# Gate-and-up weights split 256 columns at a time: products in pairs of PSUM banks, two of the four weight sums made by adding DMAs

## The chip, the core and the metric

The kernel runs on one core of one Trainium2 chip. The metric is the device time of one execution in microseconds, median of several runs. The engines are named as the profile names them: PE (TensorE matmul) with PEld (its weight load), DVE (VectorE), ACT (ScalarE), POOL (GpSimd) and SP (SyncE, which here only issues DMAs).

## What is computed

One layer of a decoder trunk on 512 tokens of width 1024, all in float32: a SwiGLU sub-layer with half weight, a mixer (causal pooling beside sliding-window attention), and a second SwiGLU sub-layer with half weight. Each sub-layer stands between two RMS norms.

```python
def swiglu(h, w_gu, w_down):
    gate, up = jnp.split(h @ w_gu, 2, axis=-1)
    return (jax.nn.silu(gate) * up) @ w_down

h = swiglu(rms_norm(x, ffn1_pre), ffn1_w_gu, ffn1_w_down)      # w_gu 1024 x 5632, w_down 2816 x 1024
x = x + 0.5 * rms_norm(h, ffn1_post)
h = token_mixer(rms_norm(x, mix_pre), cos, sin, w_in, w_pool, pool_scale, sinks, g_pool, g_attn, w_out)
x = x + rms_norm(h, mix_post)
h = swiglu(rms_norm(x, ffn2_pre), ffn2_w_gu, ffn2_w_down)
x = x + 0.5 * rms_norm(h, ffn2_post)
```

## The kernel before

**Matmuls from split operands.** Every float32 operand is split into a high part of 12 significant bits and the rest, its low part, and `mm3` (L301) makes one product from three matmuls (high by high, high by low, low by high). A split costs one copy for the high part (L125 on ACT or L127 on DVE) and one subtraction for the low part (L128, on DVE or POOL).

**Weights.** The class `Weights` (L94) holds two lists in order of use: `loads`, which SP carries out as DMAs of 512 KB into eight rotating buffers (`big`), and `todo`, the operands that are split out of them. `get(name)` (L139) splits everything up to that operand and `AHEAD` = 4 further ones; `more(n)` splits the next n, `put(hi, lo)` the next one on the engines named, and each split first sees that `run_ahead` more loads have been issued. Before the change nearly every operand is 128 partitions by 512 elements: half of a load. The pool for split weights has `WB` = 12 pairs of such tiles.

**Gate and up** (`gate_up`, L441). The 2816 columns of gate and of up are taken in eleven chunks of 256 columns (`CH`). The first chunk (c = 0) is done plainly, in eight blocks: `block(i)` for half of the tokens, gate or up, and each 128 columns; its weights are eight operands (L161 to L166), one for each of gate/up, 128 columns and half of the features. For the blocks 0 to 3 and everything that is called between them (`between`: `first_steps` L599 in the first sub-layer, `last_steps` L1115 in the second) PE, DVE, ACT and POOL keep the order of the program (`in_order`, L81). `first_steps` splits all eight operands by `put`. In the second sub-layer the last `W.more(4)` of `output` (L1094) splits the first four, and four `put`s in `last_steps` (L1120 to L1125) the other four.

The other ten chunks use seven products instead of eight of the two by two blocks (Winograd's form of Strassen's), for 128 columns at a time (`for j in range(2)`, L491): each product is twelve matmuls of 256 tokens. The operands are the four blocks of weights and four sums of them: `a11` makes two of the sums (L181, L182), `s2` (L187) and `s4` (L192) one each, on DVE; for chunk 1 POOL makes those of `a11`. The sums of tokens are made once (`token_sums`, L400). PE goes through the products 1, (4 of the block before), 2, 5, 6, 3, 7. Results are evacuated by ACT (L497, L505, L507, the silu L510) and DVE (L503, L509, L512, L484, L485). `behind` (L435) lets the splits of an operand follow the last evacuation on their engine.

**Down** (`down_proj`, L523) runs k over 22 blocks of 128 rows, with all eight PSUM banks as accumulators; the mixer and its output projection (`mixer` L938, `output` L1077) follow in an order written out by hand.

**PSUM** is one pool of eight banks (`bank`, L84).

Of the kernel before, what the change touches and what calls it, by code (L numbers as in the profile page):

```python
# [15 lines left out]
ALU = mybir.AluOpType  # L16
# [23 lines left out]
WB = 12  # L40
AB = 8
HB = 25
BIG = 8
AHEAD = 4
# [4 lines left out]
def shape_consts():  # L49
    """What depends on the shapes alone: the band of the sliding window, the count of tokens at the  # L50
    start of a trailing window, and the frequencies of the rotation."""
    c = np.zeros((P, CW), np.float32)
    i, j = np.arange(P)[:, None], np.arange(2 * P)[None, :]
    diff = i + P - j
    c[:, :256] = np.where((diff >= 0) & (diff < P), 0.0, NEG)
    for g, w in enumerate(WINDOWS):
        n = np.minimum(np.arange(16) + 1, w)
        c[:, 256 + 16 * g : 272 + 16 * g] = (np.float32(w) / n.astype(np.float32))[None, :]
    e = -np.arange(0, ROT, 2, dtype=np.float32) / np.float32(ROT)
    c[:, -8:] = np.power(np.float32(500000.0), e)[None, :]  # L60
    return c
# [3 lines left out]
def trunk_layer(  # L65
# [11 lines left out]
    pp = ctx.enter_context(tc.tile_pool(name="pp", bufs=8, space=PSUM))  # L77
# [6 lines left out]
    def bank(name):  # L84
        return pp.tile([P, 512], F32, tag="ps", name=name)
# [7 lines left out]
    # ---- weights, in the order of their use: each is split into two parts of 12 significant bits  # L93
    class Weights:  # L94
        def __init__(self):
# [3 lines left out]
            self.hi, self.lo = nc.scalar, nc.vector  # L99

        def add_load(self, key, src, shape):
            self.loads.append((key, src if isinstance(src, list) else [(slice(0, P), src)], shape))

        def add(self, name, make):
            """An operand: make() gives it in float32 once the loads added so far are there."""
            self.index[name] = len(self.todo)
            self.todo.append((name, len(self.loads), make))

        def load_to(self, n):
            while self.loaded < min(n, len(self.loads)):  # L110
                key, src, shape = self.loads[self.loaded]
                self.raw[key] = big(f"{key}_raw", shape)
                for at, part in src:
                    nc.sync.dma_start(self.raw[key][at], part)
                self.loaded += 1

        def make_to(self, n):
            while self.made < min(n, len(self.todo)):
                name, need, make = self.todo[self.made]
                self.load_to(need + self.run_ahead)  # L120
                src = make()
                hi = wp.tile(list(src.shape), F32R, tag="hi", name=f"{name}_hi")
                lo = wp.tile(list(src.shape), F32R, tag="lo", name=f"{name}_lo")
# [4 lines left out]
                self.lo.tensor_tensor(lo, src, hi.bitcast(F32), ALU.subtract)  # L128
                self.parts[name] = (hi, lo)
# [15 lines left out]
    def add_plain(key, src, shape, picks):  # L145
        W.add_load(key, src, shape)
        for name, at in picks:
            W.add(name, lambda at=at: W.raw[key][at])

    def add_gate_up(name, w_gu, c):  # L150
        def load(m, kh):
            c0 = m * FF + c * CH
            src = w_gu[0, kh * 512 : (kh + 1) * 512, c0 : c0 + CH]
            W.add_load(f"{name}_{c}{m}{kh}", src.rearrange("(k p) c -> p k c", p=P), [P, 4, CH])

        cut = [(slice(None), slice(None), slice(j * P, (j + 1) * P)) for j in range(2)]
        if c == 0:
            for m in range(2):
                load(m, 0)
                load(m, 1)  # L160
                for i in range(4):  # L161
# [3 lines left out]
                        lambda m=m, kh=kh, j=j: W.raw[f"{name}_0{m}{kh}"][cut[j]],  # L165
                    )  # L166
            return
        for m in range(2):
            for kh in range(2):
                load(m, kh)  # L170
        box = {}

        def parts(j):
            return [W.raw[f"{name}_{c}{m}{kh}"][cut[j]] for m in range(2) for kh in range(2)]

        def a11(j):
            r = parts(j)
            if j == 0:
                box["s1"] = big(f"{name}_{c}s1", (P, 4, CH))
            eng = nc.gpsimd if c == 1 else nc.vector  # L180
            eng.tensor_tensor(box["s1"][cut[j]], r[2], r[3], ALU.add)  # L181
            eng.tensor_tensor(r[2], r[0], r[2], ALU.subtract)  # L182
            return r[0]

        def s2(j):
            r = parts(j)
            nc.vector.tensor_tensor(r[0], box["s1"][cut[j]], r[0], ALU.subtract)  # L187
            return r[0]

        def s4(j):  # L190
            r = parts(j)
            nc.vector.tensor_tensor(r[1], r[1], r[0], ALU.subtract)  # L192
            return r[1]

        makers = (
            (1, a11), (2, lambda j: parts(j)[1]), (5, lambda j: box["s1"][cut[j]]), (6, s2), (3, s4),
            (7, lambda j: parts(j)[2]), (4, lambda j: parts(j)[3]),
        )
        for j in range(2):
            for p, make in makers:  # L200
                W.add(f"{name}_{c}{j}p{p}", lambda make=make, j=j: make(j))

    def add_ffn(name, w_gu, w_down):
        for c in range(NCH):
            add_gate_up(name, w_gu, c)
        for k in range(KF):
            add_plain(
                f"{name}_d{k}", w_down[0, k * P : (k + 1) * P, :], [P, D],
                [(f"{name}_d{k}{n}", (slice(None), slice(n * 512, (n + 1) * 512))) for n in range(2)],
            )  # L210

    def add_in(name, c0, w, kk, per):
        for q in range(KD // kk):
            src = w_in[0, q * kk * P : (q + 1) * kk * P, c0 : c0 + w]
            picks = [
                (f"{name}{(q * kk + i) // per}", (slice(None), i if per == 1 else slice(i, i + per)))
                for i in range(0, kk, per)
            ]
            add_plain(f"{name}_{q}", src.rearrange("(k p) c -> p k c", p=P), [P, kk, w], picks)

    # ---- what stays on chip
# [20 lines left out]
    rows = cp.tile([12, P], F32, name="rows")  # L242
# [7 lines left out]
    add_in("wq", PW, 512, 2, 1)  # L250
    add_in("wkv", 2 * PW, 256, 4, 2)
    add_in("wu", 0, 512, 2, 1)
    for n in range(2):
        ns = slice(n * 512, (n + 1) * 512)
        for q in (2, 3, 0, 1):
# [6 lines left out]
            picks = [(f"wo{n}{2 * q + i}", (slice(None), i)) for i in range(2)]  # L262
            add_plain(f"wo{n}_{q}", src, [P, 2, 512], picks)
# [12 lines left out]
    def power(ms, name):  # L276
        """ms ** -0.5"""
# [23 lines left out]
    def mm3(ps, wl, xr, first, last, open_=False):  # L301
        """ps += w.T @ x from the parts of both."""
# [10 lines left out]
    # ---- norm of a block of tokens, and its transpose  # L313
# [37 lines left out]
    def post_norm(t, parts, g, scale, name, dst=None):  # L351
        """x += scale * norm(parts) * g for a block of tokens."""
# [30 lines left out]
    def evacuate(src, t, kh, xq):  # L383
        at = slice((t % 2) * P, (t % 2 + 1) * P)
        hi, lo = xq[0][kh, t // 2]
        nc.scalar.copy(hi[:, :, at], src)
        nc.vector.tensor_tensor(lo[:, :, at], src, hi[:, :, at].bitcast(F32), ALU.subtract)

    def keep(src, t, kh, xq):
        at = slice((t % 2) * P, (t % 2 + 1) * P)  # L390
        for q in range(2):
            nc.scalar.copy(xq[1][kh, t // 2][q][:, :, at], src[:, 2 * q : 2 * q + 2, :])
# [7 lines left out]
    def token_sums(xq, name):  # L400
        """The sums of quarters that the seven products take."""
# [5 lines left out]
        for q in range(2):  # L407
            b11, b12, b21, b22 = (full[i][q] for i in ((0, 0), (0, 1), (1, 0), (1, 1)))
            nc.vector.tensor_tensor(b11, b12, b11, ALU.subtract)
            nc.vector.tensor_tensor(b12, b22, b12, ALU.subtract)  # L410
            nc.vector.tensor_tensor(b22, b22, b11, ALU.subtract)
            nc.vector.tensor_tensor(b21, b21, b22, ALU.subtract)
# [754 lines left out]
```

## Time and profile before

The profile is that of one execution on the core. A page shows the busy time of each engine; the timeline view lists instructions in order of time, merged where alike, with the idle time before them in brackets and what ended it; the windows view gives the busy time of each engine in each stretch.

| | |
|---|---|
| median of 3 runs | 871.87 us (870.04 to 873.93) |
| the profiled execution: its span from first to last instruction | 871.8 us |
| ACT busy | 428.1 us (49%) |
| POOL busy | 104.6 us (12%) |
| first sub-layer: gate and up; down | to about 242 us; 242 to about 360 us |
| mixer and output projection | about 360 to 516 us |
| second sub-layer: gate and up; down | about 516 to 745 us; 745 to 864 us |
| moved by DMA | 87.35 MB, mean 100 GB/s |

A span of 871.8 us and a median of 871.87 us say that the profiled execution is an ordinary one.

### The profile page before, as it was taken

How to read it: one execution, taken by the hardware profiler on the slowest of the kernel's cores; microseconds unless marked ns; L12 is line 12 of the kernel's file. 1: busy time of each engine (PE TensorE's matmuls, PEld its weight loads, DVE VectorE, ACT ScalarE, POOL GpSimd, SP SyncE). 2: the span in 40 equal slices, each digit the busy share in tenths (PEclk: the TensorE clock that was granted, in tenths of full speed). 3: DMA queues.
4: the chain of work that ended last, by engine and by line, in shares of the span. 5: the costliest groups of instructions: out<-in, count | busy, mean ns of one | idle time of the engine just before them, and what ended most of it. 6: DMA issues, size and time to landing. Idle time of an engine off the chain costs nothing. (4 is left out here: it accounts for less than half of the span.)

```text
span 871.8 us, 14391 instructions
## 1 busy us (share of the span) xinstructions
PE 848.6 (97%) x5633; PEld 775.9 (89%) x5633; DVE 628.8 (72%) x1177; ACT 428.1 (49%) x923; POOL 104.6 (12%) x124
## 2 busy tenths in 40 slices
PE   7999999999999999999989989999999999999996
PEld 5999999999988888888767779999999999888885
DVE  6988888888893223855998879988888888942214
ACT  6555555555583222637653356555555555832211
POOL 4300000000000000136464334000000000000000
PEclk9999999999999999999999999999999999999999
DMA  9333333333363333202023401333333333642002
GB/s 306 89 97 98 97 98 97 111 118 127 105 232 122 97 97 95 73 26 51 24 64 108 143 24 50 97 98 97 98 97 97 108 119 114 227 135 73 1 1 97
DMA packets 62448, 87.35 MB, mean 100 GB/s; under 512 B 3492, under 2 KB 50220, under 8 KB 62380
## 3 DMA queue, kind: packets, MB, share of 16 engines
q1 hardware_dynamic: 62380, 86.44, 31.0%
q8 instruction: 44, 0.72, 0.3%
q14 instruction: 24, 0.20, 0.1%
HBM read 84.33 MB, written 2.10 MB: 99 GB/s over the span
## 5 line engine op out<-in xcount | busy, mean ns | idle before, releaser
L304 PE MATMUL f_acc<-f_d_hi,f_hp_hi 128*128 128x512 f32 x352 | 137.4, 390 | 0.0
L306 PE MATMUL f_acc<-f_d_hi,f_hp_lo 128*128 128x512 f32 x352 | 137.1, 389 | 0.0
L305 PE MATMUL f_acc<-f_d_lo,f_hp_hi 128*128 128x512 f32 x352 | 137.1, 389 | 0.0
L128 DVE TENSOR_TENSOR f_d_lo<-f_d_raw,f_d_hi 128x512 fp32r<-128x512 f32 x88 | 58.9, 690 | 100.4 <-ACT f_d_hi L125 100.4
L125 ACT CAST f_d_hi<-f_d_raw 128x512 fp32r<-128x512 f32 x88 | 53.2, 621 | 108.6 <-PE f_acc L306 107.2
L304 PEld LDWEIGHTS f_acc<-f_d_hi,f_hp_hi 128*128 128x128 f32 x352 | 66.1, 188 | 13.7
L306 PEld LDWEIGHTS f_acc<-f_d_hi,f_hp_lo 128*128 128x128 f32 x352 | 66.1, 188 | 13.6
L305 PEld LDWEIGHTS f_acc<-f_d_lo,f_hp_hi 128*128 128x128 f32 x352 | 66.1, 188 | 13.6
L510 ACT ACTIVATE f_s<-f_s 128x512 f32<-128x512 f32 x40 | 25.3, 632 | 49.3 <-DVE f_s L509 49.2
L505 ACT COPY f_h<-f_y 128x256 f32<-128x256 f32 x40 | 14.9, 373 | 58.0 <-PE f_y L306 58.0
L279 POOL TENSOR_TENSOR r_f2po<-ms_f2po,half 128x1 f32<-128x1 f32 x4 | 2.2, 550 | 328.1 <-DVE ms_f2po L284 328.1
L279 POOL TENSOR_TENSOR r_f1po<-ms_f1po,half 128x1 f32<-128x1 f32 x4 | 2.2, 548 | 321.8 <-DVE ms_f1po L284 321.8
L512 DVE TENSOR_TENSOR f_h<-f_x,f_h 128x256 f32<-128x256 f32 x40 | 17.0, 424 | 31.3 <-PE f_x L306 31.3
L530 DVE TENSOR_TENSOR f_hp_lo<-f_h,f_hp_hi 128x512 fp32r<-128x512 f32 x44 | 27.9, 687 | 0.0
L192 DVE TENSOR_TENSOR f_raw<-f_raw,f_raw 128x512 f32<-128x512 f32 x40 | 27.5, 687 | 0.0
L304 PE MATMUL po<-wo_hi,yT_hi 128*128 128x512 f32 x64 | 26.4, 412 | 0.0
L305 PE MATMUL po<-wo_lo,yT_hi 128*128 128x512 f32 x64 | 25.8, 403 | 0.0
L306 PE MATMUL po<-wo_hi,yT_lo 128*128 128x512 f32 x64 | 25.7, 401 | 0.0
L507 ACT COPY f_s<-f_x 128x256 f32<-128x256 f32 x40 | 14.9, 373 | 21.9 <-PE f_x L306 21.9
L182 DVE TENSOR_TENSOR f_raw<-f_raw,f_raw 128x512 f32<-128x512 f32 x36 | 24.7, 687 | 0.0
L529 ACT CAST f_hp_hi<-f_h 128x512 fp32r<-128x512 f32 x44 | 24.6, 617 | 0.0
L298 ACT ACTIVATE j_f2po<-f_acc 128x512 bf16<-128x512 f32 x8 | 4.8, 597 | 27.3 <-PE f_acc L306 27.3
(1541 smaller groups left out, 3044.5 us busy)
## 6 DMA issues: line engine op xcount, KB each, us to landing
f_raw<-in_ffn_w_gu SPq DMA_DIRECT2D x88, 512.0 KB, 5.4
f_d_raw<-in_ffn_w_down SPq DMA_DIRECT2D x44, 512.0 KB, 4.5
x<-in_x SPq DMA_DIRECT2D x4, 512.0 KB, 8.2
wq_raw<-in_w_in SPq DMA_DIRECT2D x4, 512.0 KB, 3.6
wu_raw<-in_w_in SPq DMA_DIRECT2D x4, 512.0 KB, 3.7
wo_raw<-in_w_out SPq DMA_DIRECT2D x8, 256.0 KB, 4.0
wo_raw<-in_w_out SPq DMA_DIRECT2D x4, 512.0 KB, 3.6
out<-x SPq DMA_DIRECT2D x8, 256.0 KB, 2.1
```

The costliest lines, as they stand in the source:

```text
L125: nc.scalar.copy(hi, src)
L128: self.lo.tensor_tensor(lo, src, hi.bitcast(F32), ALU.subtract)
L182: eng.tensor_tensor(r[2], r[0], r[2], ALU.subtract)
L192: nc.vector.tensor_tensor(r[1], r[1], r[0], ALU.subtract)
L304: nc.tensor.matmul(ps, wh, xh, start=first, stop=False, skip_group_check=open_)
L305: nc.tensor.matmul(ps, wh, xlo, start=False, stop=False, skip_group_check=open_)
L306: nc.tensor.matmul(ps, wlo, xh, start=False, stop=last, skip_group_check=open_)
L505: on_act.append(nc.scalar.copy(h[:, b], py[:, a]).ins)
L510: on_act.append(nc.scalar.activation(sg, sg, AF.Silu).ins)
L512: on_dve.append(nc.vector.tensor_tensor(h[:, b], px[:, a], h[:, b], ALU.add).ins)
L529: nc.scalar.copy(hi[:, j], hs[2 * q + j])
L530: nc.vector.tensor_tensor(lo[:, j], hs[2 * q + j], hi[:, j].bitcast(F32), ALU.subtract)
```

## The change

- Chunks 1 to 10 of gate and up are split and multiplied for all 256 columns at once. An operand is now 128 partitions by 1024 elements; the tiles for split weights are twice as large and half as many (`WB` 6, `AHEAD` 2). A product runs its twelve matmuls for the first 128 columns, then for the second, into the two banks of a tile `[P, 2, 512]`, and copies and additions that read both banks become one instruction. PE's order is now 1, (4 of the chunk before), 5, 2, 6, 3, 7.
- The tokens are negated when they are copied out of their transposes, and the sums of weights are chosen so that all four are additions. Two of them are made by DMAs which POOL issues with `accum_op=ALU.add`: up's upper half of features onto its lower half (`c += d`), right behind the load of `c`, and `a += c`, behind the split of operand 6. Each is issued as two DMAs of 256 KB. The other two sums stay on DVE (one instruction each of 1024 elements), and the sums of chunk 1 leave POOL.
- PSUM: `use_banks` closes the pool and opens another, of eight single banks or of four pairs; a tile waits only for earlier users of its own banks.
- All other weights are split 1024 elements at a time, and the counts in `more` are halved. Chunk 0 still has eight operands of 512 elements, now halves of four tiles. The four `put`s are unchanged.
- The pool of 512-wide slots has 24 instead of 25.

```diff
-WB = 12
+WB = 6
-HB = 25
+HB = 24
-AHEAD = 4
+AHEAD = 2
...
+        def plus(self, key, part):
+            for k in range(0, 4, 2):
+                nc.gpsimd.dma_start(self.raw[key][:, k : k + 2], part[:, k : k + 2], accum_op=ALU.add)
...
             while self.loaded < min(n, len(self.loads)):
-                key, src, shape = self.loads[self.loaded]
+                key, src, shape, plus = self.loads[self.loaded]
                 self.raw[key] = big(f"{key}_raw", shape)
                 for at, part in src:
                     nc.sync.dma_start(self.raw[key][at], part)
+                for part in plus:
+                    self.plus(key, part)
                 self.loaded += 1
...
+        key = {i: f"{name}_{c}{i}" for i in "abcd"}
+        src = {"a": block(0, 0), "b": block(0, 1), "c": block(1, 0), "d": block(1, 1)}
+        need = {}
+        for i in "cabd":
+            need[i] = W.add_load(key[i], src[i], shape, (src["d"],) if i == "c" else ())
+        def raw(i, plus=None):
+            if plus:
+                nc.vector.tensor_tensor(W.raw[key[i]], W.raw[key[i]], W.raw[key[plus]], ALU.add)
+            return W.raw[key[i]]
+
+        for p, i, plus in ((1, "a", None), (5, "c", None), (6, "c", "a"), (2, "b", None), (7, "a", None), (3, "c", "b"), (4, "d", None)):
+            then = (lambda: W.plus(key["a"], src["c"])) if p == 6 else None
+            W.add(f"{name}_{c}p{p}", lambda i=i, plus=plus: raw(i, plus), max(need[i], need[plus or i]), then)
...
         W.run_ahead = 3
-        W.more(4)
+        W.more(2)
...
+        use_banks(f"{name}_pairs", 4)
...
         for c in range(1, NCH):
             if c == NCH - 1:
                 W.run_ahead = 2
+            nm = f"{name}_{c}p"
+            px = bank_pair(f"{name}_x{c}")
+            sg = wk.tile([P, 2, S], F32, tag="sg2", bufs=2, name=f"{name}_s{c}")
+            h = [slot(f"{name}_h{c}{j}") for j in range(2)]
+            product(px, a, operand(f"{nm}1"), xs_[1], last=False)
+            on_act.append(nc.scalar.copy(sg[:, :, a], px[:, :, a]).ins)
+            if last:
+                finish()
+                if c == NCH - 1:
+                    begin = [on_act[-2], on_dve[-1]]
+            py = bank_pair(f"{name}_y{c}")
+            product(py, a, operand(f"{nm}5"), xs_[5], last=False)
             for j in range(2):
...
+                on_act.append(nc.scalar.copy(h[j][:, b], py[:, j, a]).ins)
+            pz = bank_pair(f"{name}_z{c}")
+            product(pz, a, operand(f"{nm}2"), xs_[2])
+            on_dve.append(nc.vector.tensor_tensor(sg[:, :, a], pz[:, :, a], sg[:, :, a], ALU.add).ins)
+            product(px, a, operand(f"{nm}6"), xs_[6], False, False)
+            on_act.append(nc.scalar.copy(sg[:, :, b], px[:, :, a]).ins)
+            product(py, a, operand(f"{nm}3"), xs_[3], False)
+            on_dve.append(nc.vector.tensor_tensor(sg[:, :, b], py[:, :, a], sg[:, :, b], ALU.add).ins)
+            on_act.append(nc.scalar.activation(sg, sg, AF.Silu, scale=-1.0).ins)
+            product(px, a, operand(f"{nm}7"), xs_[7], False, False)
+            for j in range(2):
+                on_dve.append(nc.vector.tensor_tensor(h[j][:, b], px[:, j, a], h[j][:, b], ALU.add).ins)
+            last = (px, operand(f"{nm}4"), h, sg)
...
         W.lo = nc.vector
-        W.more(4)
+        W.more(2)
         for t in range(NT):
             if t == 1:
-                W.more(4)
+                W.more(2)
             pool_part(t, 0, gather(t, 0, 0))
-        W.more(4)
+        W.more(2)
         for t in range(NT):
             attn_part(t, 1, gather(t, 1, 1))
```

More of the change, by code (lines that the diff above doesn't have):

```diff
@@ L165, in add_gate_up @@
                         lambda m=m, kh=kh, j=j: W.raw[f"{name}_0{m}{kh}"][cut[j]],
+                        into=(f"{name}_c{m}{kh}", shape, cut[j]),
                     )
             return
[L168 to L201, printed above, removed]
+        key = {i: f"{name}_{c}{i}" for i in "abcd"}
[10 more added lines that the diff above has]
+            W.add(f"{name}_{c}p{p}", lambda i=i, plus=plus: raw(i, plus), max(need[i], need[plus or i]), then)
     def add_ffn(name, w_gu, w_down):
@@ L428, in product_late, with product @@
             nc.tensor.matmul(ps, w[0][:, k], xt[1][:, k], start=False, stop=last and k == 3)
-    def product(ps, w, xt, first=True, last=True):
-        for k in range(4):
-            mm3(ps, (w[0][:, k], w[1][:, k]), (xt[0][:, k], xt[1][:, k]), first and k == 0, last and k == 3, True)
+    def product(pair, half, w, xt, first=True, last=True):
+        for j in range(2):
+            at = slice(j * P, (j + 1) * P)
+            for k in range(4):
+                mm3(
+                    pair[:, j, half], (w[0][:, k, at], w[1][:, k, at]), (xt[0][:, k], xt[1][:, k]),
+                    first and k == 0, last and k == 3, True,
+                )
     @contextmanager
@@ new lines, in gate_up @@
+            on_act.append(nc.scalar.activation(sg, sg, AF.Silu, scale=-1.0).ins)
+            product(px, a, operand(f"{nm}7"), xs_[7], False, False)
+            for j in range(2):
+                on_dve.append(nc.vector.tensor_tensor(h[j][:, b], px[:, j, a], h[j][:, b], ALU.add).ins)
+            last = (px, operand(f"{nm}4"), h, sg)
+        h, sg = last[2:]
+        product(pz, b, last[1], xs_[4])
+        for j in range(2):
+            nc.vector.tensor_tensor(h[j][:, b], h[j][:, b], sg[:, j, b], ALU.mult)
+            on_act.append(nc.scalar.copy(h[j][:, a], px[:, j, a]).ins)
@@ L531, in h_pair, with in_halves @@
             hparts[q] = (hi, lo)
+        def in_halves(w):
+            return [tuple(part[:, n * 512 : (n + 1) * 512] for part in w) for n in range(2)]
         acc = {(t, n): bank(f"{name}_acc{t}{n}") for t in range(NT) for n in range(2)}
@@ L545, in down_proj @@
                     h_pair(k // 2 + 1)
-                w = [W.get(f"{name}_d{k}{n}") for n in range(2)]
+                w = in_halves(W.get(f"{name}_d{k}"))
             for t in range(NT):
@@ L553, in down_proj @@
                 h_pair(k // 2)
-            tail.append([W.get(f"{name}_d{k}{n}", 0) for n in range(2)])
+            tail.append(in_halves(W.get(f"{name}_d{k}", 0)))
         if name == "f1":
             W.run_ahead = 3
-            W.more(4)
+            W.more(2)
         for t in range(NT):
@@ L988, in mixer @@
         run(1)
-        W.more(2)
+        W.more(1)
         attn_rms(0)
@@ L1003, in mixer @@
         attn_out(2)
-        W.more(2)
+        W.more(1)
         pool_mid(2)
```

181 lines of the change are left out of this document (91 added, 90 removed).

## Prediction

> **What bounds the kernel now.** I read the page first: its first lines and the busy time of the engines.
>
> ```profile
> span 871.8 us, 14391 instructions
> ...
> PE 848.6 (97%) x5633; PEld 775.9 (89%) x5633; DVE 628.8 (72%) x1177; ACT 428.1 (49%) x923; POOL 104.6 (12%) x124
> ```
>
> PE is busy for all but 23 us, so the question is where those lie. The windows view cut by stage tells it; the columns are PE, PEld, DVE, ACT and POOL busy with their counts, PE's granted clock, the DMA share and GB/s.
>
> ```profile
> 0.00:25.00 25.00, 20.48 (x122) 15.89 (x123) 17.65 (x30) 13.71 (x33) 13.07 (x18) 0.93 0.95 300
> ...
> 50.00:240.00 190.00, 190.00 (x1586) 190.00 (x1585) 162.40 (x314) 104.14 (x212) 0.00 (x0) 1.00 0.34 109
> ...
> 425.00:450.00 25.00, 22.54 (x108) 17.07 (x107) 24.72 (x62) 17.20 (x48) 12.48 (x18) 0.93 0.07 22
> 450.00:475.00 25.00, 23.13 (x102) 17.94 (x100) 22.09 (x32) 9.76 (x17) 12.28 (x11) 0.93 0.43 127
> ...
> 500.00:525.00 25.00, 19.92 (x118) 17.37 (x117) 18.75 (x32) 14.24 (x39) 8.71 (x10) 0.93 0.07 22
> 525.00:550.00 25.00, 24.36 (x201) 23.81 (x200) 24.56 (x35) 15.49 (x33) 9.29 (x7) 1.00 0.14 43
> 550.00:741.00 191.00, 191.00 (x1594) 191.00 (x1593) 163.39 (x308) 104.18 (x211) 0.00 (x0) 1.00 0.33 106
> ```
>
> In the two gate-and-up loops (50 to 240 and 550 to 741 us) PE never rests: 1586 matmuls in 190 us, 0.1198 us each. DVE is at 162.4 of 190 us there and makes nobody wait. The change rewrites these loops, and there is nothing in them to win; what can change is the idle time around them, in the start, in the mixer and its output (425 to 525 us), and in the start of the second sub-layer. A window with clock 0.93 lost 0.07 x 25 = 1.75 us to a lower clock, and the three after 400 us are those where PE rests most.
>
> **The loops: 0 us.** The matmuls stay: seven products of 24 for 256 columns, 24 x 0.1198 = 2.87 us each, 20.1 us a chunk. The groups of instructions (count, busy us, mean ns) give DVE and ACT:
>
> ```profile
> L192 DVE TENSOR_TENSOR f_raw<-f_raw,f_raw 128x512 f32<-128x512 f32 x40 | 27.5, 687 | 0.0
> L503 DVE TENSOR_TENSOR f_s<-f_z,f_s 128x256 f32<-128x256 f32 x40 | 16.9, 422 | 0.0
> L128 DVE TENSOR_TENSOR f_20p_lo<-f_raw,f_20p_hi 128x512 fp32r<-128x512 f32 x12 | 8.1, 686 | 0.0
> L125 ACT CAST f_20p_hi<-f_raw 128x512 fp32r<-128x512 f32 x12 | 7.0, 619 | 1.1 <-DVE f_raw L192 1.1
> L497 ACT COPY f_s<-f_x 128x256 f32<-128x256 f32 x40 | 14.6, 366 | 3.8 <-PE f_x L306 3.8
> ```
>
> DVE before, per chunk: 2 x (4 sums + 7 low parts) x 0.687 + 10 x 0.42 = 19.3 us. From 256 to 512 elements costs 0.265 us, so 1024 take about 1.22: after, 9 x 1.22 + 2 x 0.69 + 6 x 0.42 = 14.9 us. ACT goes from 12.2 to about 10.9 us by the same reckoning (0.253 more per 256 elements, 1.12 for 1024). Both engines get lighter, and PE gains nothing.
>
> What could cost is the adding DMA `a += c`. It may start when operand 6's sum has read `a`; that sum is queued behind the last additions after product 7 of the chunk before, so counted from the start of product 1: 2 x 0.42 + 1.22 = 2.1 us, or 4.5 us if operand 5's two parts go first. It must have landed before operand 7 is split, and operand 3 stands behind operand 7 on ACT; product 3 starts at 5 x 2.87 = 14.35 us and needs two high parts and a low one before (2 x 1.12 + 1.22 = 3.5), so by 10.9 us. That leaves 6.4 to 8.8 us. No adding DMA is in this trace. Plain loads, median us from issue to landing, and over the 88 loads of gate and up the time of SP's issue (ns, least/median/most) and the range of landings:
>
> ```profile
> f_raw<-in_ffn_w_gu SPq DMA_DIRECT2D x88, 512.0 KB, 5.4
> wo_raw<-in_w_out SPq DMA_DIRECT2D x8, 256.0 KB, 4.0
> ...
> L114 SPq DMA_DIRECT2D f_raw<-in_ffn_w_gu x88: 367/368/2199, 2.6 to 715.6; - x88
> ...
> DMA to landing us min/median/max: 3.5/5.4/10.5
> ```
>
> Bounds: 3.5 us (as the quickest load) and 10.5 (as the slowest). Two halves of 4.0 us a little apart are near 5.4, which I take: it lands in time. The other end would make every chunk late by up to 10.5 - 6.4 = 4.1 us. `c += d` is issued nearly a chunk ahead; its 20 us cover it.
>
> **The first start: 0 us (-1.3 to +2).** In the order of the program POOL now issues `c += d` of chunk 1 before it makes the root for the third block of tokens (`root_of(2)`), and it must wait for that load, the first of four issued from 9.62 on.
>
> ```profile
> 9.62 5.63 SPq L114 DMA_DIRECT2D f_raw<-in_ffn_w_gu  x4
> 18.50 0.66 POOL L279 TENSOR_TENSOR r_a<-ms_a,half 128x1 f32<-128x1 f32 x1 [1.16 <-DVE ms_a L284]
> 22.27 3.46 DVE L323 SCALAR_TENSOR_TENSOR xn_a<-x,r_a,g 128x512 f32<-128x512 f32 x2 [0.45 <-POOL r_a L279]
> 22.70 1.04 PE L378 MATMUL tr_f<-ident,xn_a 128*128 128x128 f32 x8
> 23.58 3.29 POOL L181 TENSOR_TENSOR f_1s<-f_raw,f_raw 128x512 f32<-128x512 f32 x2
> 31.05 0.74 PE L428 MATMUL f_c<-f1b_lo,f_c_hi 128*128 128x256 f32 x4 [0.68 <-DVE f1b_lo L387]
> ```
>
> With the slowest landing (10.5) the load is there by 20 us. Issuing a DMA on POOL isn't in the trace; SP's took 0.37 at least and 2.2 at most among its 88 loads, and I take 1 us. The root then comes at about 22 instead of 18.50, and the transposes at 22.70 wait about 1 us. Against that, POOL's sums of chunk 1 (L181) go; beside them two instructions of DVE took 3.46 us, and PE's 0.68 us wait at 31.05 goes with them. These cancel.
>
> **Output projection: -3.8 us.** Here the halved counts matter. In `output` the third `W.more` split four operands of the second sub-layer's chunk 0. Now it splits two, although these are still 512 wide. DVE, in order:
>
> ```profile
> 488.04 1.24 DVE L127 CAST f_c_hi<-f_raw 128x512 fp32r<-128x512 f32 x1
> ...
> 493.06 0.42 DVE L127 CAST f_c_hi<-f_raw 128x512 fp32r<-128x512 f32 x1
> ...
> 495.18 0.74 DVE L1053 SCALAR_TENSOR_TENSOR hm<-po,rpt,hm 128x512 f32<-128x512 f32 x1
> ...
> 503.61 1.86 PE L378 MATMUL tr_f<-ident,xn_c 128*128 128x128 f32 x8 [3.29 <-DVE xn_c L323]
> ```
>
> The third and fourth split (493.06 to 495.18) go, so the addition at 495.18, which heads the chain to the transposes at 503.61, comes 2.1 us earlier and PE's 3.29 us wait shrinks to 1.2. With so short a rest I expect the lower clock of that window to go too, another 1.7 us: together -3.8 (-2.1 to -5).
>
> **Start of the second sub-layer: +7.2 us.** The two splits come due later. The four `put`s now make operands 3 to 6 of chunk 0 instead of 5 to 8, and 7 and 8 are made by `get` inside blocks 2 and 3, with the last `put`'s engines: high part on DVE, low part on POOL, both in program order.
>
> ```profile
> 521.12 0.37 PE L425 MATMUL f_c<-f2b_hi,f_c_hi 128*128 128x256 f32 x1
> 523.17 0.69 DVE L128 TENSOR_TENSOR f_c_lo<-f_raw,f_c_hi 128x512 fp32r<-128x512 f32 x1
> 524.34 1.42 POOL L128 TENSOR_TENSOR f_c_lo<-f_raw,f_c_hi 128x512 fp32r<-128x512 f32 x1 [2.98 <-DVE ms_c L284]
> 524.64 1.67 DVE L128 TENSOR_TENSOR f_c_lo<-f_raw,f_c_hi 128x512 fp32r<-128x512 f32 x1
> 525.72 1.00 POOL L279 TENSOR_TENSOR r_c<-ms_c,half 128x1 f32<-128x1 f32 x1
> 527.78 1.16 PE L378 MATMUL tr_f<-ident,xn_c 128*128 128x128 f32 x8
> 528.42 1.28 DVE L387 TENSOR_TENSOR f2b_lo<-tr_f,f2b_hi 128x512 fp32r<-128x512 f32 x2
> 528.64 1.29 POOL L128 TENSOR_TENSOR f_c_lo<-f_raw,f_c_hi 128x512 fp32r<-128x512 f32 x1 [1.92 <-PE tr_f L378]
> 530.21 0.28 PE L425 MATMUL f_c<-f2b_hi,f_c_hi 128*128 128x256 f32 x1
> ```
>
> On the clock of before: block 1 started at 521.12 and now waits for operand 3 (low part from 523.17, done 523.86). Its second half waits for operand 4, whose low part POOL ends at 524.34 + 1.42 = 525.76, and lasts 12 x 0.12 = 1.44 us, to 527.2. Block 2's first half finds operand 5 (done 526.31): to 528.65. Its second half needs operand 7: high part behind the evacuations of 528.42 to 529.70, with 0.42 to 530.1; low part on POOL behind the root (to 526.72), two DMA issues and operand 6's low part (to 529.93): 530.1 + 1.29 = 531.4. It ends at 532.85. The transposes (0.92 from 527.78 to the next matmul's start) and block 3's first half end at 535.2; operand 8 waits for ACT's copy and DVE's evacuations of these transposes (533.8 + 0.62 + 1.28 = 535.7), then 0.42 + 1.29: 537.4. Block 3 ends at 538.85; before, its second half started at 530.21 and ended at 531.65. Difference 7.2 us (5 to 9: DVE and POOL also slow one another, 0.69 against 1.67 above). Nothing takes it back, since the loop runs at PE's pace.
>
> **Lower clock there: +1.7 us (0 to 3.4).** PE now rests three times for 2 to 3 us. In this trace 3.29 us of rest stood beside a loss of 1.75; I take one such loss.
>
> **The rest: +0.3 us.** A pair of banks may wait for the multiplication of chunk 0 that reads one of them.
>
> ```profile
> 543.50 0.28 PE L304 MATMUL f_x<-f2b_hi,f_10p_hi 128*128 128x256 f32 x1
> 548.19 0.68 DVE L470 TENSOR_TENSOR f_h<-f_c,f_s 128x512 f32<-128x512 f32 x1
> ```
>
> Product 5 would start at 543.50 + 2.87 = 546.4 and that multiplication ended at 548.87, so 0 to 2.5 us in each sub-layer; with four pairs to choose from I stay near 0. Of one slot less and of larger splits in the mixer the trace says little (-2 to +2): 0.
>
> **Sum:** 871.8 + 0 + 0 - 3.8 + 7.2 + 1.7 + 0.3 = 877.2, say **877 us**. The span of the profiled execution stands 0.1 below the median, so nothing is added.
>
> **A rule that speaks against the change.** The rows show that DVE and POOL hold one another off: the same low part takes 0.69 us alone and 1.67 beside POOL. If POOL's issuing of DMAs is held off in the same way, each of the two issues in each start loses up to 1 us more, and the roots and low parts behind them: +2 in the first start, +2 in the second, 881. [...]
>
> **Rivals.** (1) *The adding DMA is late* in every chunk: 1.5 us, between 0 and 4.1, in each of 20 chunks: 907. For it: landings up to 10.5. Against: the median of 5.4. (2) *The relief wins*: the first two `put`s come early enough. They stand behind the last residual on DVE, the end of the chain that the output's splits delayed; if that chain gains 5 us and the waits of blocks 1 to 3 come to less than that (short waits, no lower clock, POOL free of sums: 3 us), the time is 871.8 - 5 + 3 = 870, not slower than before; it decides as soon as the waits fall below the gain. Against it: block 1 itself moves up with the chain, so its 2.7 us stay. (3) *POOL's issues are held off*, as worked out above: 881.
>
> **Chances.** Forecast 0.60, (1) 0.13, (2) 0.17, (3) 0.10. A change of about 0.5%, 4.4 us, is what a measurement of this kernel can tell from none, so slower begins at 876.2, which the forecast's own spread (871 to 883) passes in five cases of eight: slower 0.38 + 0.13 + 0.08 = 0.59; same 0.22 + 0.12 + 0.02 = 0.36; faster, mostly from (2), 0.05. The range is 868 to 890: it takes in (2), (3) and the unknown costs, and leaves out most of (1).
>
> **What would show it.** Loops with PE full and DVE near 75% confirm the zero; idle PE before f_y or f_x there, ended by ACT or a DMA, is rival (1). The transposes of 503.61 should come some 2 us earlier, and the blocks of f2's chunk 0 should show waits for f_c_lo on DVE, then twice on POOL. If these waits are missing, the step on the second start is wrong, and with it the sign.

## The result: slower by 15.6%, four fifths of it in the two loops

The changed kernel takes 1007.48 us (median of 4, 1004.50 to 1013.12), the kernel before beside it 872.54 (870.04 to 873.93): a ratio of 1.1558, 95% interval 1.1517 to 1.1599. The forecast was 877 us, 868 to 890. The direction was right and the size was not: 131 us too little.

The first lines and the busy time of the engines on the page of the changed kernel:

```profile
span 1011.1 us, 14000 instructions
...
PE 901.9 (89%) x5633; PEld 820.6 (81%) x5633; DVE 558.5 (55%) x823; ACT 395.3 (39%) x671; POOL 189.5 (19%) x190
```

DVE and ACT did get lighter (628.8 and 428.1 us before), and PE has as many matmuls as before. But PE now rests for 109 us of the span, not for 23, and its busy time has grown by 53 us with the same work: the granted clock is 0.91 in the first loop, not 1.00. The windows view by stage (PE, PEld, DVE, ACT, POOL busy with counts, granted clock, DMA share, GB/s):

```profile
50.00:240.00 190.00, 166.23 (x1249) 162.83 (x1249) 102.60 (x125) 73.23 (x93) 36.51 (x30) 0.91 0.55 123
...
575.00:600.00 25.00, 9.16 (x57) 8.12 (x55) 14.24 (x20) 5.79 (x14) 10.74 (x11) 0.77 0.57 137
650.00:800.00 150.00, 129.59 (x957) 126.99 (x956) 78.65 (x96) 54.51 (x70) 28.00 (x23) 0.90 0.55 126
```

Where the kernel before ran 1586 matmuls in 190 us, this one runs 1249; in the second start (575 to 600) PE is busy for little more than a third. One chunk takes 190 / (1249 / 168) = 25.6 us, not 20.1. The loss per chunk has two parts: idle PE, (190 - 166.23) / 7.43 = 3.2 us, and the clock, 0.09 x 190 / 7.43 = 2.3 us. The sum, 5.5 us, over 20 chunks is 110 us.

From the starts of the first matmuls on PE's timeline I divide both executions, and four of the experiments below, into stages (us; "first start" ends and each loop begins with product 1 of chunk 1, "second start" begins with the first product of chunk 0, the last row ends with PE's last matmul). The profiled executions are 1011.1 and 871.8 us long, so 139 us are to be explained:

| stage | before | after | room | pinned | pair_first | predicted change |
|---|---|---|---|---|---|---|
| first start | 40.3 | 46.4 | 41.5 | 38.1 | 39.3 | 0 |
| loop 1 | 201.8 | 258.6 | 207.2 | 207.9 | 204.6 | 0 |
| down projection, mixer, output | 274.3 | 268.4 | 269.4 | 268.7 | 271.5 | -3.8 |
| second start | 27.1 | 53.3 | 43.5 | 37.5 | 28.3 | +8.9 and 0.3 |
| loop 2 | 201.6 | 257.7 | 205.2 | 204.3 | 202.4 | 0 |
| second down projection | 119.5 | 120.1 | 120.1 | 120.1 | 120.0 | 0 |

What PE waited for, in the view of the waits cut to PE (us in total, times, longest). There are nine rows "f_y L315 <- ACT", one for each of chunks 2 to 10 with both sub-layers in it; the largest and the smallest are shown. They add up to 47 us, and the rows "f_y L317 <- DVE" of the same chunks to 15:

```profile
PE f_c L440 <- POOL f_c_lo L164: 17.4, 2, 14.1
PE tr_f L389 <- DVE xn_a L334: 9.6, 4, 5.9
PE f_y L315 <- ACT f_8p_hi L161: 6.8, 2, 3.7
...
PE f_y L315 <- ACT f_4p_hi L161: 4.4, 2, 2.3
...
PE f_y L317 <- DVE f_4p_lo L164: 1.9, 2, 0.9
```

Of these rows only that of the transposes (`tr_f`) stood in the kernel before, with 3.6 us in total and 1.5 at most. The matmuls of f_y on line 315 that wait for ACT are the start of product 3. The timeline of chunk 3 in the first sub-layer, rows of four engines in order of time, tells why:

```profile
93.19 1.23 DVE L215 TENSOR_TENSOR f_3c_raw<-f_3c_raw,f_3a_raw 128x1024 f32<-128x1024 f32 x1
95.06 1.21 POOL L141 DMA_DIRECT2D f_3a_raw<-in_ffn_w_gu  x1 [9.04 <-DVE f_3c_raw L215]
99.65 1.22 POOL L141 DMA_DIRECT2D f_3a_raw<-in_ffn_w_gu  x1 [3.37 <-issue]
105.26 1.04 ACT L161 CAST f_3p_hi<-f_3a_raw 128x1024 fp32r<-128x1024 f32 x1 [5.38 <-DMA f_3a_raw<-in_ffn_w_gu]
106.21 1.04 ACT L161 CAST f_3p_hi<-f_3c_raw 128x1024 fp32r<-128x1024 f32 x1
107.30 0.58 PE L315 MATMUL f_y<-f1b_hi,f_3p_hi 128*128 128x256 f32 x1 [2.35 <-ACT f_3p_hi L161]
108.75 0.58 PE L317 MATMUL f_y<-f1b_hi,f_3p_lo 128*128 128x256 f32 x1 [0.65 <-DVE f_3p_lo L164]
109.13 0.42 PE L315 MATMUL f_y<-f1b_hi,f_3p_hi 128*128 128x256 f32 x1
...
109.78 0.41 PE L315 MATMUL f_y<-f1b_hi,f_3p_hi 128*128 128x256 f32 x1
...
114.53 0.28 PE L315 MATMUL f_x<-f1t_hi,f_3p_hi 128*128 128x256 f32 x1
...
114.89 0.28 PE L315 MATMUL f_x<-f1t_hi,f_3p_hi 128*128 128x256 f32 x1
```

Read it from the top. Operand 6's sum releases `a` at 94.42. POOL issues the first half of `a += c` at 95.06 and the second half only at 99.65. In the 3.37 us between, the profile shows nothing that POOL waits for ("issue"), but the landings tell: the first half landed at 99.33, 0.32 us before the second was issued, and in all 40 pairs of this execution the second half is issued 0.26 to 0.33 us after the first has landed. `a` is complete at 105.26, 10.8 us after the sum. Operand 7 is cast then, operand 3 stands behind it on ACT at 106.21, and product 3 starts 2.35 us late. Its matmuls then follow one another at (109.78 - 109.13) / 3 = 0.217 us; the granted clock from 109 to 113 is 0.50, and by 114.53 they are back at 0.12. That second price, the clock, was in none of the prediction's numbers for a late DMA.

The second start, POOL's and PE's timeline:

```profile
583.64 1.26 POOL L141 DMA_DIRECT2D f_1c_raw<-in_ffn_w_gu  x1
589.68 1.22 POOL L141 DMA_DIRECT2D f_1c_raw<-in_ffn_w_gu  x1 [4.78 <-issue]
590.44 1.75 POOL L164 TENSOR_TENSOR f_c_lo<-f_raw,f_c_hi 128x512 fp32r<-128x512 f32 x1
594.23 1.22 POOL L141 DMA_DIRECT2D f_2c_raw<-in_ffn_w_gu  x1 [2.04 <-issue]
598.99 1.20 POOL L141 DMA_DIRECT2D f_2c_raw<-in_ffn_w_gu  x1 [3.55 <-issue]
599.75 1.75 POOL L164 TENSOR_TENSOR f_c_lo<-f_raw,f_c_hi 128x512 fp32r<-128x512 f32 x1
601.55 0.58 PE L440 MATMUL f_c<-f2b_hi,f_c_lo 128*128 128x256 f32 x1 [14.11 <-POOL f_c_lo L164]
```

The low parts of chunk 0 wait on POOL behind four DMA issues that take 16 us. The prediction had two issues there at 1 us each.

### The profile page after: what moved, and what is told of

It reads as the page before. It is cut to its first block, busy times and chain, and to the rows that moved or that the text cites. A ratio compares the mean times of both kernels' runs of the same rounds, so it can differ in the third digit from the quotient of the medians.

```text
span 1011.1 us, 14000 instructions
## 1 busy us (share of the span) xinstructions
PE 901.9 (89%) x5633; PEld 820.6 (81%) x5633; DVE 558.5 (55%) x823; ACT 395.3 (39%) x671; POOL 189.5 (19%) x190
## 5 line engine op out<-in xcount | busy, mean ns | idle before, releaser
L315 PE MATMUL f_acc<-f_d_hi,f_hp_hi 128*128 128x512 f32 x352 | 137.3, 390 | 1.2 <-DVE f_h L550 1.2
L317 PE MATMUL f_acc<-f_d_hi,f_hp_lo 128*128 128x512 f32 x352 | 137.0, 389 | 0.0
L164 DVE TENSOR_TENSOR f_d_lo<-f_d_raw,f_d_hi 128x1024 fp32r<-128x1024 f32 x44 | 53.6, 1223 | 90.8 <-ACT f_d_hi L161 90.8
L161 ACT CAST f_d_hi<-f_d_raw 128x1024 fp32r<-128x1024 f32 x44 | 46.1, 1053 | 100.3 <-PE f_acc L317 100.3
L315 PEld LDWEIGHTS f_acc<-f_d_hi,f_hp_hi 128*128 128x128 f32 x352 | 66.1, 188 | 15.0 <-PE pcols L741 0.9
L317 PEld LDWEIGHTS f_acc<-f_d_hi,f_hp_lo 128*128 128x128 f32 x352 | 66.1, 188 | 13.8
L539 ACT ACTIVATE f_s<-f_s 128x1024 f32<-128x1024 f32 x20 | 21.2, 1060 | 85.3 <-DVE f_s L538 85.3
L523 ACT COPY f_s<-f_x 128x512 f32<-128x512 f32 x20 | 11.8, 589 | 64.8 <-PE f_x L317 64.8
L440 PE MATMUL f_c<-f2b_hi,f_c_lo 128*128 128x256 f32 x64 | 18.6, 317 | 17.7 <-POOL f_c_lo L164 17.4
L538 DVE TENSOR_TENSOR f_s<-f_y,f_s 128x512 f32<-128x512 f32 x20 | 13.8, 691 | 33.8 <-PE f_y L317 33.8
L440 PEld LDWEIGHTS f_c<-f2b_hi,f_c_lo 128*128 128x128 f32 x64 | 14.0, 219 | 18.4 <-POOL f_c_lo L164 17.8
L315 PE MATMUL po<-wo_hi,yT_hi 128*128 128x512 f32 x64 | 25.3, 395 | 0.0
L317 PE MATMUL po<-wo_hi,yT_lo 128*128 128x512 f32 x64 | 24.9, 390 | 0.0
```

Source lines behind the costliest of these rows:

```text
L161: nc.scalar.copy(hi, src)
L315: nc.tensor.matmul(ps, wh, xh, start=first, stop=False, skip_group_check=open_)
L317: nc.tensor.matmul(ps, wlo, xh, start=False, stop=last, skip_group_check=open_)
L440: nc.tensor.matmul(ps, w[1][:, k], xt[0][:, k], start=False, stop=False)
L538: on_dve.append(nc.vector.tensor_tensor(sg[:, :, b], py[:, :, a], sg[:, :, b], ALU.add).ins)
L539: on_act.append(nc.scalar.activation(sg, sg, AF.Silu, scale=-1.0).ins)
```

## The experiments

Theory 1: the two halves of an adding DMA go one after the other because both do not fit in the room that the kernel gives POOL's DMAs, and this makes `a += c` late. Rivals: POOL needs the time by itself to write each DMA; the 256-column operands and the pairs of banks are late for reasons of their own; the adding traffic slows everything. A single execution stands behind each number unless an interval is given.

### room: more room for POOL's DMAs

```diff
-HB = 24
+HB = 23
...
-    nc = _bacc.Bacc("TRN2", ..., dynamic_dma_scratch_size=1024)
+    nc = _bacc.Bacc("TRN2", ..., dynamic_dma_scratch_size=2048)
```

One slot of `hp` is given up to make place for the room. In the trace PE, DVE, ACT and POOL go through the same instructions in the same order as before.

> Theory 1 (room): the second half of an adding DMA is not issued before the first has landed, because both do not fit into the room that the kernel gives POOL's DMAs (dynamic_dma_scratch_size=1024). With 2048 the second issue follows the first within 1.5 us instead of 4.67, a + c has landed some 7 us after the sum that releases it instead of 10.6, product 3 waits no more, and the matmuls run at the full clock again: about 100 us less in the loops and 5 to 10 in the two starts, 890 to 910. Theory 2 (preparation): POOL needs 3.5 us of its own to write each DMA, whatever the room: 1007 as before, the second issue still 4.7 us after the first. Theory 3 (pairs): the 256-column operands themselves are late: 1007.

Measured: 895.64 us, 112 less than the changed kernel. Chunk 3 on the timeline of this run:

```profile
82.03 1.23 DVE L215 TENSOR_TENSOR f_3c_raw<-f_3c_raw,f_3a_raw 128x1024 f32<-128x1024 f32 x1
83.90 2.45 POOL L141 DMA_DIRECT2D f_3a_raw<-in_ffn_w_gu  x2 [7.48 <-ACT f_s L523]
90.67 1.05 ACT L161 CAST f_3p_hi<-f_3a_raw 128x1024 fp32r<-128x1024 f32 x1 [1.94 <-DMA f_3a_raw<-in_ffn_w_gu]
```

Both halves are now one row of two, back to back, 2.45 us together. `a` is complete 7.4 us after the sum (90.67 - 83.26) instead of 10.8. The window of the first loop:

```profile
50.00:240.00 190.00, 188.32 (x1554) 186.65 (x1553) 129.25 (x167) 88.69 (x112) 41.73 (x34) 1.00 0.69 152
```

PE is full again but for 1.7 us, at the full clock (the whole loops still take 5.4 and 3.6 us longer than in the kernel before). Theory 1 stands; "preparation" falls, since the same DMAs are issued by the same POOL with no gap between. The same bytes are added by the same DMAs, so the traffic was not what slowed everything. DVE is denser beside them than in the changed kernel (68% of the window instead of 54%), so DVE did not hold the issues off either.

### slot: the control

```diff
-HB = 24
+HB = 23
```

> Control for room: one slot less (HB 23), the room for POOL's DMAs as in the changed kernel (1024). If the room was what the run before it showed, nothing changes: 1003 to 1012, the second half 4.7 us behind the first. If the slot count did it, some 896.

Measured: 1017.35, a little above what was expected. Its timeline shows the gap as before:

```profile
96.31 1.21 POOL L141 DMA_DIRECT2D f_3a_raw<-in_ffn_w_gu  x1 [8.71 <-DVE f_3c_raw L215]
101.14 1.22 POOL L141 DMA_DIRECT2D f_3a_raw<-in_ffn_w_gu  x1 [3.62 <-issue]
```

The slot gains nothing; the room did it.

### swap and room_swap: operand 3 ahead of operand 7

```diff
-..., (2, "b", None), (7, "a", None), (3, "c", "b"), (4, "d", None)):
+..., (2, "b", None), (3, "c", "b"), (7, "a", None), (4, "d", None)):
```

> Operand 3 is split ahead of operand 7; the DMAs stay as they are. Theories 1 and 2: only operand 7 needs the adding DMA, and it is used 2.87 us later than operand 3, so the wait of 2.4 to 3.7 us before product 3 goes and at most 1 us stays before product 7; clock back at full: 900 to 915, with both starts still late. Theory 3 (pairs): no change, 1007.

> Room of 2048 and operand 3 split ahead of operand 7. Of the 895.6 us of the run with the room alone, its loops lose 2.2 us (f1, 50 to 225 us) and 4.1 us (f2) in waits of 0.1 to 0.8 us for low parts of operands 2 and 3. Theory 1: with 7 out of 3's way those at product 3 go, 888 to 893. If the waits are DVE's load and not the DMA's, they stay: 895.

Measured: 956.45 and 935.88; both expectations missed, and the second kernel is 40 us slower than room alone. Product 3 no longer waits in either. Something else does, DVE and PE in swap:

```profile
111.42 0.76 DVE L542 TENSOR_TENSOR f_h<-f_x,f_h 128x256 f32<-128x256 f32 x2 [2.18 <-PE f_x L317]
112.09 1.22 DVE L164 TENSOR_TENSOR f_4p_lo<-f_4a_raw,f_4p_hi 128x1024 fp32r<-128x1024 f32 x1
113.36 0.39 PE L317 MATMUL f_x<-f1b_hi,f_4p_lo 128*128 128x256 f32 x1 [1.54 <-DVE f_4p_lo L164]
```

This is product 1 of the next chunk. Operands are made two ahead of the product that asks. With the two entries exchanged, product 3 no longer reaches operand 1 of the next chunk; it is made one product later, and its low part stands on DVE behind the additions after product 7. I had moved a second thing without seeing it.

### swap_lead: the same with the lead kept

```diff
-                return W.get(name)
+                return W.get(name, AHEAD + (name[-1] == "3"))
```

> The room stays at 1024; operand 3 ahead of 7 as in the run swap, and product 3 asks for three operands ahead, so that operand 1 of the next chunk is split one product earlier again. If swap lost only its lead (1.7 us before product 1 in every chunk, and the lower clock behind it), both loops come near 202 to 208 us each with the adding DMA as late as ever, and only the starts stay: 897 to 912. If a late a + c still decides, waits before product 7 show up instead: 930 or more.

Measured: 933.53, the second branch. The wait is now at product 7, in 13 of the chunks. The view of PE's waits names ACT's copy on line 536; on ACT that copy (103.25 in chunk 3) stands behind the split of operand 7, which waited for the DMA:

```profile
PE f_x L315 <- ACT f_s L536: 8.7, 13, 1.5
...
102.30 1.05 ACT L161 CAST f_3p_hi<-f_3a_raw 128x1024 fp32r<-128x1024 f32 x1 [5.56 <-DMA f_3a_raw<-in_ffn_w_gu]
```

With the small room a late `a += c` still decides, 2.87 us later.

### dve_a and dve_both: the sums on DVE

```diff
+            if i == "a" and plus:
+                nc.vector.tensor_tensor(W.raw[key[i]], W.raw[key["c"]], W.raw[key[plus]], ALU.subtract)
...
-(7, "a", None)
+(7, "a", "d")
...
-            then = (lambda: W.plus(key["a"], src["c"])) if p == 6 else None
+            then = None
```

dve_both also makes c + d on DVE, for which d is loaded ahead of b.

> a + c is made by DVE (as c+d+a minus d), c + d still by the adding DMA. Theories 1 and 2: nothing waits for a late DMA in the loops, DVE has 16.1 of 20.1 us a chunk: 895 to 910, the two starts still late by some 25 us. Theory 3 (pairs): waits before product 3 stay, over 980. Were the adding traffic itself the cost (theory 4), half of it stays: about 950.

> Both sums by DVE, no adding DMA at all; the grouping by 256 columns and the pairs of banks stay. Theories 1, 2 and 4: loops at full pace and the first start as before the change; of the predicted second start (+7.2, lower clock +1.7) and output (-3.8) the sum stays: 873 to 885. Theory 3 (pairs): over 980.

Measured: 913.72, 4 us above its range, and 910.56, 26 above. In dve_a the loops take 210 and 208 us and the starts stay late (46.9 and 50.4). In dve_both the second start falls to 37.6 us, but the loops take 217 each:

```profile
50.00:225.00 175.00, 165.91 (x1368) 164.28 (x1368) 131.08 (x154) 77.73 (x96) 0.00 (x0) 1.00 0.32 100
```

PE's wait before product 2 of chunk 3 in it, alike in chunks 2 to 9:

```profile
PE f_z L319 <- DVE f_3p_lo L164: 2.3, 2, 1.1
```

No pair of banks and no 256-column operand keeps PE waiting for 3 us in every chunk here, and none stands before product 3, so that rival falls. But DVE at 75% is late once a chunk all the same: its two more sums stand in front of operand 2's low part. The adding DMAs do relieve DVE where it counts.

### late_sum, later and pinned: POOL's queue in the starts

late_sum issues c + d of chunk 1 behind the last low part of chunk 0; later issues that of every next chunk behind operand 2; pinned also ties each adding DMA behind the one before it. All have the larger room.

```diff
-            then = (lambda: W.plus(key["a"], src["c"])) if p == 6 else None
+            if p == 2 and c < NCH - 1:
+                then = lambda: W.plus(f"{name}_{c + 1}c", block(1, 1, c + 1))
...
         def plus(self, key, part):
+            with behind(self.tail):
...
+            self.tail = [ins]
```

> Room of 2048; the adding DMA c + d of chunk 1 is issued after the last low part of chunk 0 instead of at its load, in both sub-layers. If POOL's queue (the DMAs ahead of roots and low parts) is what the two starts lose, the waits of 6.9 and 1.9 us in the second start shrink to about 1.7 together (as the steps of the prediction have them without the issues) and that of 1.9 in the first to under 1: 886 to 889. If the low parts on POOL are late for another reason (DVE's order, the two splits that moved), no more than 2 us.

> Room of 2048; each adding DMA c + d is issued after operand 2 of the chunk before (chunk 1: after the last operand of chunk 0), so no adding DMA stands ahead of roots or low parts in POOL's queue in either start. Then the second start, from the first product of chunk 0 to the first of chunk 1, takes what the prediction worked out, 27.1 + 7.2 + 1.7 = 36 us, where late_sum had 40.8: 884 to 888. If it stays at 40, POOL's queue isn't what is left there.

> As later, but each adding DMA is tied behind the one before it on POOL, since the planner had still put the DMA of chunk 2 ahead of a root and a low part in the second start. Now no adding DMA stands ahead of them: if POOL's queue is what made the second start longer than the prediction's 36 us (later: 41.8), it comes to 34 to 38, 884 to 888. If it stays above 40, the moved splits alone cost more than the 7.2 us that the prediction gave them.

Measured: 891.19, 891.99 and 884.99. The first start fell at once, from 41.5 to 38.1 us. In the second start the first two missed: the sum of chunk 2 was still issued ahead of a low part, in late_sum at its load, in later by the planner (which orders an engine's instructions where the program doesn't). POOL in later:

```profile
528.78 1.27 POOL L164 TENSOR_TENSOR f_c_lo<-f_raw,f_c_hi 128x512 fp32r<-128x512 f32 x1 [1.92 <-issue]
532.50 2.50 POOL L141 DMA_DIRECT2D f_2c_raw<-in_ffn_w_gu  x2 [2.46 <-DMA f_2c_raw<-in_ffn_w_gu]
534.06 2.24 POOL L164 TENSOR_TENSOR f_c_lo<-f_raw,f_c_hi 128x512 fp32r<-128x512 f32 x1
```

and in pinned (its line 167 is line 164 of the others):

```profile
526.93 1.30 POOL L167 TENSOR_TENSOR f_c_lo<-f_raw,f_c_hi 128x512 fp32r<-128x512 f32 x1 [1.92 <-DVE f_c_hi L166]
528.64 2.12 POOL L167 TENSOR_TENSOR f_c_lo<-f_raw,f_c_hi 128x512 fp32r<-128x512 f32 x1 [0.42 <-issue]
```

With no DMA ahead the second low part follows after 0.42 us, not 4.0. The second start is 37.5 us; the prediction's own steps had 27.1 + 8.9 = 36.0. dve_both, which has no adding DMA at all, had 37.6.

### mended, later_more, later_more_swap, pinned_more_swap

These have the larger room and split four operands of chunk 0 at the third place of the output again. mended adds swap and the late first sum, later_more is later with the four, later_more_swap adds operand 3 ahead of 7 with its lead, pinned_more_swap ties the DMAs.

```diff
             pool_part(t, 0, gather(t, 0, 0))
-        W.more(2)
+        W.more(4)
```

> Room of 2048, operand 3 ahead of 7, the late first sum, and the third place of the output split four operands of chunk 0 again, as before the change. Loops at full pace, both starts and the output as in the kernel before: 868 to 876 beside 872.2. Above 880 means that the starts lose for a reason not yet named.

> As later, with four operands of chunk 0 split at the third place in the output again. By the prediction's terms that undoes +7.2, +1.7 and -3.8 to -4.7: 878 to 882, the second start near 28 us, and the wait before the transposes in the output back (2 to 3.5 us). If the moved splits weren't the cause of the second start, no change.

> As later_more, with operand 3 ahead of 7 and the lead kept: the loops at full pace (202 us each instead of 205 to 208): 868 to 875 beside 872. If the waits of 0.1 to 0.8 us are DVE's load rather than the adding DMA, they stay: 878 to 882.

> later_more_swap (880.2) with the adding DMAs tied in order. Its second start waits 3.4 us for the normed block (POOL's root behind a DMA and beside a low part of 1024 elements on DVE) and 5.6 us for the banks of chunk 0's multiplication, behind the landing of c + d of chunk 1. If the DMA ahead of the root is the first, that wait falls to about 1.5; the second stays, since chunk 1's DMA is not issued earlier: 876 to 880. If the root is held by DVE alone, 880.

| run | us (median of 4) | ratio to before, 95% |
|---|---|---|
| mended | 926.31 | 1.0582 (1.0534 to 1.0629) |
| later_more | 890.08 | 1.0202 (1.0174 to 1.0230) |
| later_more_swap | 880.23 | 1.0103 (1.0070 to 1.0137) |
| pinned_more_swap | 880.58 | 1.0090 (1.0069 to 1.0112) |

mended still has the lost lead of swap in it. later_more gave 2 us where at least 10 were expected: the second start fell from 41.8 to 34.6, while the output grew by 2.9 and loop 2 by 1.9. later_more_swap missed its range too, and its loops take 205.0 and 204.3 us, not the 202 expected: but for their two ends, where some 3 us go, they run at PE's full pace, with no wait before product 3. The first loop:

```profile
50.00:225.00 175.00, 175.00 (x1460) 175.00 (x1460) 120.94 (x149) 85.74 (x106) 41.16 (x34) 1.00 0.70 153
```

What is left in it stands in two rows of PE's waits:

```profile
PE f_x L319 <- DVE f_h L495: 5.6, 1, 5.6
PE tr_f L393 <- DVE xn_c L338: 5.6, 2, 3.4
```

pinned_more_swap takes the second down to 2.6, 2, 2.3, of which 0.3 us lies in the second start, and the first to 4.8. Its median, 880.58, stayed where it was, at the edge between its two branches.

### pool_sum and pair_first: the last wait

pool_sum is pinned_more_swap with c + d of chunk 1 as an ordinary addition on POOL, tied behind POOL's last low part. pair_first then ties the parts of three token sums behind chunk 0's multiplications:

```diff
+        with behind([silu, mult]):
+            split_sums((6, 7, 4))
```

> As pinned_more_swap, with c + d of chunk 1 by an ordinary addition on POOL, as the kernel before had it, in place of its adding DMA (later chunks keep theirs). If the 5.6 us are the landing of that DMA, on which the split of operand 5 and behind it chunk 0's multiplication wait, they fall to 1 to 2: 870 to 876. If they are the pair of banks or the order on DVE and ACT, they stay: 877 to 881.

> As pool_sum, with the parts of the token sums 6, 7 and 4 tied behind chunk 0's silu and multiplications on ACT and DVE. In pool_sum the multiplication that frees the pair of banks for product 1 starts 3.3 us after the last product of chunk 0 in the second sub-layer, behind five of these parts and a weight sum, and PE waits 3.8 us (in the first sub-layer 1.6). If the pair waits for DVE's order, the wait falls to 1 to 2 us there and to 0 to 1 in the first: 872 to 875, no difference from before that can be told. If it is the banks themselves (the products that used them), no change: 877.

Measured: 876.79 (ratio 1.0055, 1.0033 to 1.0076) and 874.33 (median of 10; ratio 1.0006, 0.9987 to 1.0026, beside 872.41). pool_sum's time lies between its two branches and tells little. In the profiled executions its second start is 1.1 us shorter than that of pinned_more_swap, but the stage of down projection, mixer and output, which the edit does not touch, is 4.1 us shorter (268.4 instead of 272.5), at a granted clock of 1.00 instead of 0.98. What raised the clock there is not shown; in pair_first the stage is back at 271.5. The wait tells more: it fell only from 4.8 to 3.8, so the landing was the smaller part of it; DVE and PE there:

```profile
538.53 1.89 DVE L442 TENSOR_TENSOR f2t_lo<-f2f,f2t_hi 128x512 fp32r<-128x512 f32 x3
540.34 1.22 DVE L222 TENSOR_TENSOR f_1c_raw<-f_1c_raw,f_1b_raw 128x1024 f32<-128x1024 f32 x1
541.47 1.29 DVE L442 TENSOR_TENSOR f2t_lo<-f2f,f2t_hi 128x512 fp32r<-128x512 f32 x2
542.67 0.69 DVE L500 SCALAR_TENSOR_TENSOR f_h<-f_c,f_s 128x512 f32<-128x512 f32 x1
543.41 0.39 PE L324 MATMUL f_x<-f2b_hi,f_1p_hi 128*128 128x256 f32 x1 [3.80 <-DVE f_h L500]
```

The multiplication that frees the pair stood behind five parts and a weight sum that nobody needed yet. With them behind it the second start is 28.3 us, and this wait is down to 0.8. This last version cannot be told from the kernel before. Nothing run here is faster than the kernel before.

## Why the prediction was wrong, step by step

- **The loops: 0 us. This step failed, with 113 of the 139 us.** It priced `a += c` by single loads on SP's queue and took "two halves of 4.0 us a little apart" as 5.4 us from issue to landing. One half does land in such a time (median 4.6, below), but the second half is issued when the first has landed: 10.2 us from first issue to `a` complete, 10.8 from the sum. The slack of 6.4 to 8.8 us was right: 94.42 to 104.95, where product 3 was due, less its 3.5 us of splits, is 7.0.
- **Rival (1), the adding DMA late in every chunk,** was the case that came: its place and its mechanism were right, its price (1.5, at most 4.1 us) was not. The wait is 3.0 us in chunk 3 and 3.2 on average, inside the bound, and the lower clock behind it costs 2.3 more, which the price left out. Even with the larger room the slack is thin: in room product 3 waits up to 0.6 us in some chunks, and in later_more_swap, with operand 3 ahead of 7 as well, not at all. Its chance of 0.13 was low for a term whose own row was missing, priced from rows of another queue.
- **The first start: 0 us, measured +6.1.** The same cause. The root came at 26.54 behind two issues, at 19.41 and 25.78, not at 22, and the transposes waited 5.9 us. The wait of 0.68 us went, as forecast, and with the larger room and the late sum (late_sum, later, pinned) this start takes 38.1 us, 2 less than before. Whether that is the relief of POOL that the step weighed against it is not shown: dve_both, which relieves POOL of these sums too, has 40.5.
- **The output: -3.8, right.** From the matmuls of `py` at 440.31 (now 501.96) to the transposes PE takes 59.2 us instead of 63.3, -4.1: the 3.29 us wait in front of them is gone, and one of 0.9 stands before the next ones. Behind them, up to the second start, the clock is 1.00 instead of 0.87, as forecast, but new waits take most of that back: 12.2 us instead of 12.8. Of the whole stage (-5.9) another 1.2 us, ahead of this stretch, was not predicted.
- **The second start: +8.9, measured +26.2.** The splits that moved cost about what was worked out: with the DMAs out of their way (pinned) it is +10.4, of which some 6.4 us are more idle PE (forecast 7.2, and 0.3 for the pairs) and some 3.4 a granted clock of 0.91 (forecast 1.7, at most 3.4). The rest is the DMAs' 16 us on POOL, where 2 us had been put. So the sign was right for the reason given, but that reason makes up some 10 of the 139 us.
- **The pairs: +0.3.** In the changed kernel 0.9 us of wait; where other waits go it comes up to 3.8 and 5.6, above the bound of 2.5, until DVE's order is mended (pair_first).
- **Rival (3), issues held off by DVE,** did not happen in this form: all 80 issues of the changed kernel take 1.20 to 1.36 us, where up to 1 us more than the 1 us taken had been reckoned from two rows of low parts, and with the larger room two follow one another in 2.45 us beside a busy DVE (room). What held the second one was the first: it is issued 0.26 to 0.33 us after the first has landed. **Rival (2)** was out of reach: the output and the stretch behind it gain 4.7 us, and the second start costs 10.4 even without DMAs in its way.

## What to carry to other kernels

Price an operation by the queue that will run it, and ask how many of it fit there at once: the two halves of `a += c`, which did not fit together here, went one after the other, 10.2 us for both in chunk 3, though the median of one half was 4.6. Where PE rests in every chunk, look at the clock beside the wait: in the changed kernel 3.2 us of rest a chunk stood beside 2.3 us lost to the clock. And before two entries of an order are exchanged, ask what else is counted by their places.

## What the runs showed of the chip that was not expected

The adding DMAs of the changed kernel, from the view of line 141 (one row of POOL's issues with the duration in ns, least, median and most; then issue to landing in us over all 80 halves of 256 KB):

```profile
L141 POOL DMA_DIRECT2D f_3a_raw<-in_ffn_w_gu x4: 1213/1218/1222, 95.1 to 679.7; - x4
...
DMA to landing us min/median/max: 4.1/4.6/7.8
```

Adding costs little more than loading: 4.6 us against 3.8 to 4.0 for a plain 256 KB load (of the output's weights). What costs is the room: in chunk 3, with a `dynamic_dma_scratch_size` of 1024, the second issue comes 4.6 us after the first (4.8 in slot), 0.32 us after the first has landed; with 2048 (room) both issues together take 2.45 us. That a second adding DMA waits for the landing of the first when the room is small is what the changed kernel, room and slot show.

Beside short rests that came back every chunk the clock was lower in some runs and not in others: at a wait of 1.1 us a chunk (dve_both) it stayed at 1.00, and at 3.0 (after) it was 0.91. At 1.5 it went either way. In swap it was 0.97; in room_swap the same 1.54 us stood before product 1 of chunks 2 to 10, and the clock held for 125 us and then fell:

```profile
75.00:225.00 150.00, 140.71 (x1112) 138.31 (x1111) 91.60 (x109) 61.74 (x79) 31.44 (x26) 0.97 0.62 138
...
50.00:175.00 125.00, 115.76 (x945) 113.69 (x944) 79.83 (x97) 52.85 (x66) 27.00 (x22) 1.00 0.65 146
175.00:265.00 90.00, 85.38 (x665) 84.35 (x664) 56.31 (x78) 40.24 (x55) 14.72 (x12) 0.94 0.55 132
```

The first row is of swap, the other two of room_swap. So the length of a rest alone did not decide; what else did is not shown.

DVE and POOL slowed one another with larger operands too. In later_more_swap a low part of 128x1024, 1.22 us alone, took 3.52 beside a low part and a root on POOL, and that root, 0.99 us in pinned and 1.00 in pool_sum, took 2.48:

```profile
525.42 3.52 DVE L164 TENSOR_TENSOR f_1p_lo<-f_1a_raw,f_1p_hi 128x1024 fp32r<-128x1024 f32 x1 [0.32 <-ACT f_1p_hi L161]
```
